# Letting an account of the array's use order TensorE's queue ahead of the experts of a hybrid block

## The chip, the core and the metric

The kernel runs on one core of a Trainium2 chip. Its engines work side by side and are tied by semaphores: TensorE (PE in the rows; PEld are its weight loads), VectorE (DVE), ScalarE (ACT), GpSimd (POOL), and SyncE (SP), which issues nearly all transfers. Each engine works through its own queue in order. The metric is the device time of one execution in microseconds (us).

## What is computed

One decoder block on 256 tokens of width 1024, in float32. One projection of x feeds an RWKV-7 time mixing (8 heads of 64), an attention (8 heads of 64) and two gates per channel; their gated sum goes through `w_out`, a residual and a layer norm. Then each token goes to 4 of 32 experts, each with 12 MB of weights.

```python
proj = jnp.einsum('btd,dc->btc', x, w_in)          # 5376 columns: rwkv 1792, attention 1536, gates 2048
y_rwkv = rwkv7_time_mix(p_rwkv, ...) @ w_branch_rwkv
y_attn = moba_attention(q, k, v) @ w_branch_attn
merged = gates[:, :, 0] * y_rwkv + gates[:, :, 1] * y_attn
x = layer_norm(DEEPNORM_ALPHA * x + merged @ w_out, ln1_g, ln1_b)
x = layer_norm(DEEPNORM_ALPHA * x + moe_ffn(x, ...), ln2_g, ln2_b)   # top 4 of 32 experts
```

The recurrence of the time mixing runs over time, `S = S * w + (S @ -kk) (kk * a) + v k`; the kernel does it in two blocks of 128 tokens, for which the inverse of a triangular 128 x 128 matrix per head and block is needed.

## The kernel before

**Stages.** The mixer comes first, to about 246 us of the profiled execution; then the branch products, `w_out`, the first norm, the router and the gathering, to about 303 us; then the experts, two to a pair, whose weights stream through a ring of ten slots (21 pieces of 1 MB), and a short end with the second norm. The slots are carved from memory that the mixer uses until its tiles are free; `stream(n)` issues the transfers up to the n-th piece, on SP's queue. The last slots become free when the output products and the router are done.

**Products of x.** The projection is made in 21 jobs of 256 columns. For a job, 2 x 512 KB of `w_in` are fetched into `wr` (four buffers), and each half is split into a high and a low part (`wh` by ACT, L211; `wl` by POOL for the first half and DVE for the second, L212; three buffers each). Then come 16 steps of three matmuls (`three`; rows `g<-xh,wh`, `g<-xl,wh`, `g<-xh,wl` or with the operands the other way round). Each step ends in `yield 0.0`.

**Half 0 and half 1 of the RWKV heads** (`rwkv_half`): decay and gates, the norm of k (a product with `bones` in `cf`), the transposes of v, b and k (`w<-ident,va`, `w<-ident,bk`), four units that make the masked 128 x 512 score blocks `sc_t` (two matmul groups, two masked copies by DVE, L531, each; a unit takes two of the four buffers of `work()`), the inverse of 16 x 16 blocks by a chain of substitution steps on DVE (L542 to L558) and four copies by ACT (L561), its transposes (`w<-ident,ring` or `w<-ident,kr`), the merges of blocks 16 to 32, 32 to 64 and 64 to 128 (many small matmuls of 64 x 32 to 64 x 64, L583 to L623), the state in two steps b = 0 and 1 (L628 to L682), and the head norm (two products with `cf`, the second for the variance; root by ACT, L698; reciprocals and products by DVE, L702 to L704). Half 1 may not begin its units before half 0's state is done.

**Attention** runs in two halves as well: per pair of heads the scores (`a<-ak,aq`), the softmax on DVE and ACT (L736 to L743), the transposes of the scores (`a<-ident,sm`), a copy by ACT (L749) and the weighted sums (`a<-sm,rope_t`).

**What sets the order.** These are Python generators: half 0, half 1, attention, and the jobs of products (`gemms`). Each `yield` gives back a number of us until the generator may go on, from the table `WAIT`, or a job and a wait after it. A loop (L828 to L847) runs the first generator that is ready by a clock of its own, `spent`, to which every matmul adds its planned time (`mm`, `turned_`); when two steps of the first three have run in a row (`FILL`), a step of products goes next. Every instruction on TensorE is tied behind the one before (`queued`). When no generator is ready, `spent` jumps. `next_job` keeps the last gate job until the first three generators are done, fetches a job's weights and, by `done` times, calls `stream`. DVE, ACT and POOL get their work in an order that follows from this program.

Of the kernel before, what the change touches and what calls it, by code (L numbers as in the profile page):

```python
# [9 lines left out]
F32 = mybir.dt.float32  # L10
# [28 lines left out]
        "sm": 3.6, "tr": 0.81, "s1": 13.02}  # L39

FILL = 2

EARLY_GATES = 3
LATE_GATES = 1
# [75 lines left out]
def hybrid_block_kernel(ctx: ExitStack, tc: tile.TileContext, A, out):  # L120
# [139 lines left out]
    ea, sq, kk, k2 = (half_t[:, i * 512:(i + 1) * 512] for i in range(4))  # L260


    def mm(out, lhsT, rhs, **k):
        n = int(np.prod(rhs.shape[1:]))
        if rhs.dtype != F32:
            spent[0] += n / 2400
        elif rhs.shape[0] <= 64:
            spent[0] += max(n, 64) / 1200
        else:
            spent[0] += max(n, int(np.prod(lhsT.shape[1:]))) / 600  # L270
        return queued("pe", nc.tensor.matmul, out, lhsT=lhsT, rhs=rhs, **k)

    def turned_(out, in_, identity):
        spent[0] += 0.107
        return queued("pe", nc.tensor.transpose, out=out, in_=in_, identity=identity)

# [136 lines left out]
    def rwkv_half(hf):  # L413
# [169 lines left out]
        for h in range(2):  # L583
# [1 line left out]
            for u in range(8):  # L585
                mm(pz[hv[h], u * 32:(u + 1) * 32], lhsT=sc_t[hv[h], u, hv[h]], rhs=first_cols(xm, h)[:, u], start=True, stop=True)
            nc.scalar.copy(out=first_cols(zt, h), in_=quarter(pz, hv[h], 32).rearrange("p u (g s) -> p u g s", s=16))
        yield WAIT["mg"]
        for h in range(2):
            pxt, px = work(), work()  # L590
            for u in range(8):
                mm(pxt[hv[h], u * 32:(u + 1) * 32], lhsT=zt[hv[h], u, hv[h]], rhs=second_cols(xt, h)[:, u], start=True, stop=True)

            n = 2 - h
            r = slice(64 * h, 64 * h + 32 * n)
            for u in range(8):
                mm(px[r, u * 16 * n:(u + 1) * 16 * n], lhsT=xt[hv[h], u, r], rhs=first_cols(zt, h, n)[:, u], start=True, stop=True)
            mask = cm[r, None, M_LEV + 64 * h:M_LEV + 64 * h + 32 * n].rearrange("p u (g s) -> p u g s", s=32)[:, :, :, 0:16]
            nc.vector.copy_predicated(out=first_cols(xm[r], 0, n) if h == 0 else xm[r, :, 64:80].rearrange("p u (g s) -> p u g s", s=16), mask=mask.to_broadcast([32 * n, 8, n, 16]), data=quarter(px, r, 16 * n).rearrange("p u (g s) -> p u g s", s=16))
            mask = cm[hv[h], None, M_LEV + P + 64 * h:M_LEV + P + 64 * h + 64].rearrange("p u (g s) -> p u g s", s=32)[:, :, :, 16:32]  # L600
            nc.vector.copy_predicated(out=second_cols(xt, h), mask=mask.to_broadcast([64, 8, 2, 16]), data=quarter(pxt, hv[h], 32).rearrange("p u (g s) -> p u g s", s=16))
        yield WAIT["mg2"]

        for size, pairs in ((32, 2), (64, 1)):
            lo_ = [slice(2 * size * g, 2 * size * g + size) for g in range(pairs)]
            hi_ = [slice(2 * size * g + size, 2 * size * g + 2 * size) for g in range(pairs)]
            for g in range(pairs):
                pz = work()
                for u in range(8):
                    mm(pz[hi_[g], u * size:(u + 1) * size], lhsT=sc_t[lo_[g], u, hi_[g]], rhs=xm[lo_[g], u, lo_[g]], start=True, stop=True)  # L610
                nc.scalar.copy(out=zt[hi_[g], :, lo_[g]], in_=quarter(pz, hi_[g], size))
            yield WAIT["mg"]
            for g in range(pairs):
                pxt = work()
                for u in range(8):
                    mm(pxt[lo_[g], u * size:(u + 1) * size], lhsT=zt[hi_[g], u, lo_[g]], rhs=xt[hi_[g], u, hi_[g]], start=True, stop=True)
                if size == 32 and g == 0:
                    px = work()
                    for u in range(8):
                        mm(px[hi_[g], u * size:(u + 1) * size], lhsT=xt[hi_[g], u, hi_[g]], rhs=zt[hi_[g], u, lo_[g]], start=True, stop=True)  # L620
                    nc.vector.tensor_copy(out=xm[hi_[g], :, lo_[g]], in_=quarter(px, hi_[g], size))
                nc.scalar.copy(out=xt[lo_[g], :, hi_[g]], in_=quarter(pxt, lo_[g], size))
            yield WAIT["mg"]  # L623

        late_a, late_b = (buf(n).rearrange("p (i c) -> p i c", i=2) for n in ("va2", "bk"))
        y_t, sq2, rstd, yn = (t[:, i, :] for t in (late_a, late_b) for i in range(2))
# [197 lines left out]
    def at(n):  # L824
        r = ready[n]
        return done.get(r[0], 1e9) + r[1] if isinstance(r, tuple) else r

    tasks = [rwkv_half(0), second_half(), halves_of(attention_half), gemms()]  # L828
    ready = [0.0] * 4
    since = 0  # L830
    while min(at(n) for n in range(3)) < 1e9 or "gate7" not in done:
        n = min((n for n in range(4) if at(n) <= spent[0]), default=None)
        if n is None:
            spent[0] = min(at(n) for n in range(4))
            continue
        if n < 3 and since >= FILL and at(3) <= spent[0]:
            n = 3
        wait = next(tasks[n], 1e9)
        since = 0 if n == 3 else since + 1
        if wait is None and min(at(i) for i in range(3)) <= spent[0]:  # L840
            wait = 0.0
        if wait is None:

            spent[0] = max(spent[0], min(at(n) for n in range(3)))
            wait = 0.0
        ready[n] = wait if isinstance(wait, tuple) else spent[0] + wait
# [776 lines left out]
```

## Time and profile before

| | us |
|---|---|
| median of 3 runs | 1240.23 |
| lowest, highest | 1227.66, 1240.44 |
| the profiled execution | 1235.69 |
| its span, first to last instruction | 1233.8 |

| share of the span | PE | PEld | DVE | ACT | POOL |
|---|---|---|---|---|---|
| busy | 93% | 47% | 33% | 21% | 8% |

[...] The profile cuts the span into slices of 31 us; the first ten are the mixer, the branches and the router, the other thirty the experts. A busy share there mixes stages with different limits, so the rows below are taken stage by stage: windows give the busy time of each engine and the granted clock of a stretch, timelines the instructions of one engine in order of time, with the idle time before them and what ended it.

### The profile page before, as it was taken

To read this page: it belongs to the slowest core of one execution; us is meant where nothing else is said; L and a number is where in the kernel's file an instruction comes from. 1 tells how busy PE (TensorE), PEld (TensorE's weight loads), DVE (VectorE), ACT (ScalarE), POOL (GpSimd) and SP (SyncE) were. 2 spreads that over 40 slices of the span, in tenths; PEclk is the share of its full clock that TensorE was granted. 3 is DMA by queue.
4 is the path that set the end of the run, shared out by engine and by line. 5 is a ranking of instruction groups with operands and counts; after the bars stand their busy time and mean duration, and the time that the engine had idled before them with its cause. 6 is when DMAs were issued, how large, how long until landed. Compare 5 with 4: busy or idle time off the path is not lost.

```text
span 1233.8 us, 15101 instructions
## 1 busy us (share of the span) xinstructions
PE 1147.7 (93%) x6396; PEld 582.5 (47%) x6396; DVE 403.3 (33%) x767; ACT 264.0 (21%) x486; POOL 97.0 (8%) x75
## 2 busy tenths in 40 slices
PE   9889979999999999999989887799998998989996
PEld 7778869888334343433424223234342333333323
DVE  6974693385522223122202011112112121212123
ACT  7455425544111110101111000011010101010111
POOL 3321121152300000000000000000000000000001
PEclk9998899999999999999999998899999999999999
DMA  8434145487999999999999999999999999999993
GB/s 269 128 95 151 56 153 172 156 318 277 397 428 427 427 426 427 429 426 427 429 427 427 428 426 426 427 427 428 427 429 426 427 428 428 428 426 427 427 420 130
DMA packets 62271, 439.79 MB, mean 356 GB/s; under 512 B 5662, under 2 KB 34168, under 8 KB 37528
## 3 DMA queue, kind: packets, MB, share of 16 engines
q1 hardware_dynamic: 60904, 427.18, 84.4%
q0 software_dynamic: 864, 11.27, 2.3%
q8 instruction: 52, 0.85, 0.3%
q10 hardware_dynamic: 432, 0.33, 0.1%
q14 instruction: 19, 0.16, 0.0%
HBM read 437.71 MB, written 1.05 MB: 356 GB/s over the span
## 4 chain that ended last, share of the span: by engine, by line
issue 34%; DMA 31%; PE 25%; DVE 7%; ACT 1%; POOL 1%; SPq 0%; POOLq 0%; ACTq 0%; DVEq 0%
DMA ring<-in_expert_w_in_dram 19%; DMA ring<-in_expert_w_out_dram 10%; PE w L132 7%; PE g L132 6%; PE h L132 5%; PE y L132 3%; PE a L132 2%; PE t L132 1%; DVE ring L554 1%; DMA acc<-in_expert_b_in_dram 1%; DVE wl L212 1%; PE t L1118 1%; DMA wr<-in_w_out_by_rows_dram 1%; DVE m L132 0%; POOL acc L1217 0%
## 5 line engine op out<-in xcount | busy, mean ns | idle before, releaser
L132 PE MATMUL h<-ring,xg 128*64 128x512 f32 x2048 | 461.4, 599 | 26.0 <-DMA ring<-in_expert_w_in_dram 25.2
L132 PEld LDWEIGHTS h<-ring,xg 128*64 128x64 f32 x2048 | 143.6, 137 | 308.8 <-issue 282.1
L132 PE MATMUL y<-ring,at 128*64 128x512 f32 x992 | 223.3, 599 | 22.8 <-DMA ring<-in_expert_w_out_dram 20.9
L1317 DVE TENSOR_SCALAR h<-h 128x512 f32<-128x512 f32 x32 | 22.4, 700 | 386.6 <-PE h L132 386.6
L132 PEld LDWEIGHTS y<-ring,at 128*64 128x64 f32 x992 | 69.2, 137 | 163.7 <-issue 134.4
L1318 ACT ACTIVATE lc<-h 128x512 f32<-128x512 f32 x32 | 19.1, 597 | 501.2 <-DVE h L1317 501.2
L132 PE MATMUL g<-xh,wh 128*128 128x256 f32 x304 | 95.4, 314 | 2.8 <-ACT rope_s L710 2.1
L1352 DVE TENSOR_TENSOR acc<-acc,t 128x512 f32<-128x512 f32 x56 | 38.5, 688 | 167.9 <-PE t L132 167.9
L132 PE MATMUL g<-xh,wl 128*128 128x256 f32 x304 | 87.9, 289 | 1.7 <-DVE wl L212 1.5
L132 PE MATMUL g<-xl,wh 128*128 128x256 f32 x304 | 87.3, 287 | 0.0
L1341 ACT COPY yp<-y 64x512 f32<-64x512 f32 x62 | 35.9, 579 | 207.6 <-PE y L132 207.0
L132 PEld LDWEIGHTS g<-xh,wh 128*128 128x128 f32 x304 | 59.4, 195 | 12.4 <-issue 8.1
L1118 PE MATMUL t<-oh,x 128*128 128x128 f32 x480 | 59.0, 282 | 6.3 <-DVE oh L1104 6.3
L1118 PEld LDWEIGHTS t<-oh,x 128*128 128x128 f32 x480 | 56.2, 196 | 18.1 <-issue 17.7
L132 PEld LDWEIGHTS g<-xl,wh 128*128 128x128 f32 x304 | 59.5, 196 | 2.2 <-issue 2.2
L132 PEld LDWEIGHTS g<-xh,wl 128*128 128x128 f32 x304 | 59.4, 195 | 2.4 <-DVE wl L212 1.7
L132 PE MATMUL t<-yp,ct 128*128 128x512 f32 (+1 forms) x124 | 56.5, 598 | 0.7 <-ACT yp L1341 0.7
L212 POOL TENSOR_TENSOR wl<-wr,wh 128x1024 fp32r<-128x1024 f32 x18 | 43.2, 2400 | 139.5 <-ACT wh L211 126.4
L211 ACT CAST wh<-wr 128x1024 fp32r<-128x1024 f32 (+1 forms) x44 | 42.2, 969 | 46.7 <-PE g L132 34.5
L132 POOL TENSOR_TENSOR acc<-acc,x 128x256 f32<-128x256 f32 x4 | 3.9, 992 | 486.9 <-DVE ln_rs L132 486.8
L132 PEld LDWEIGHTS t<-yp,ct 128*128 128x128 f32 x124 | 22.3, 189 | 34.5 <-issue 32.3
L1121 ACT ACTIVATE xg<-t,gbc 128x128 f32<-128x128 f32 x60 | 27.4, 457 | 42.4 <-PE t L1118 24.8
(375 smaller groups left out, 1075.7 us busy)
## 6 DMA issues: line engine op xcount, KB each, us to landing
ring<-in_expert_w_in_dram SPq DMA_DIRECT2D x122, 2048.0 KB, 37.0
ring<-in_expert_w_out_dram SPq DMA_DIRECT2D x61, 2048.0 KB, 39.1
wr<-in_w_in_dram SPq DMA_DIRECT2D x40, 512.0 KB, 3.9
ring<-in_expert_w_in_dram POOLq DMA_DIRECT2D x5, 2048.0 KB, 30.1
wr<-in_w_out_by_rows_dram SPq DMA_DIRECT2D x8, 512.0 KB, 4.8
ring<-in_expert_w_out_dram SPq DMA_DIRECT2D x4, 1024.0 KB, 26.4
wr<-in_w_branch_attn_dram SPq DMA_DIRECT2D x4, 512.0 KB, 7.3
wr<-in_w_branch_rwkv_dram SPq DMA_DIRECT2D x4, 512.0 KB, 9.3
```

The costliest lines, as they stand in the source:

```text
L132: queues[e] = make(*a, **k)
L211: nc.scalar.copy(out=hi[:, sl], in_=raw[:, sl])
L212: engine.tensor_tensor(out=lo[:, sl], in0=raw[:, sl], in1=hi[:, sl].bitcast(F32), op=ALU.subtract)
L554: nc.vector.tensor_tensor(out=pr[:, 0:m, 0:n], in0=nn[:, j + 1:SUB, j:j + 1].to_broadcast([P, m, n]), in1=xb[:, j:j + 1, 0:n].to_broadcast ...
L1118: last = nc.tensor.matmul(ps[:, i * ns:(i + 1) * ns], lhsT=x1[:, b, k * P:(k + 1) * P], rhs=oh[:, b, :], start=b == 0 and i == 0, stop=b = ...
L1121: def scaled(ps, n, k0, put=lambda e, make, **a: make(**a)):
L1317: nc.vector.tensor_scalar(out=gate_, in0=gate_, scalar1=7.0, scalar2=None, op0=ALU.min)
L1318: nc.scalar.activation(out=lc4, in_=g4, func=AF.Sigmoid, scale=1.702)
L1341: nc.scalar.copy(out=yp[r0_:r0_ + CAP, dh * 512:(dh + 1) * 512], in_=y[dh * CAP:(dh + 1) * CAP, :])
L1352: nc.vector.tensor_tensor(out=acc[:, b, hs], in0=acc[:, b, hs], in1=ps, op=ALU.add)
```

## The change

The planner now keeps a list of what each matmul uses of the array: in `mm`, the planned time of its columns times the share of the 128 x 128 array that its operands fill; in `turned_`, the time of a transpose. `in_use()` sums the list over the last `STRETCH` us of the planner's clock and divides by `STRETCH`. When a step of the halves or the attention is due and `in_use()` is below `FULL`, a step of products goes first, unless the last try found the products dry. Beside that, the merges have more and shorter steps: each half or pair of blocks now ends with a `yield` of its own, with a wait of 0 except the last.

```diff
+STRETCH = 3.4
+FULL = 0.65
...
+    def in_use():
+
+        while used and used[0][0] < spent[0] - STRETCH:
+            used.pop(0)
+        return sum(u for _, u in used) / STRETCH
+
     def mm(out, lhsT, rhs, **k):
         n = int(np.prod(rhs.shape[1:]))
+        m = int(np.prod(lhsT.shape[1:]))
+        used.append((spent[0], n / (600 if rhs.dtype == F32 else 2400) * min(rhs.shape[0] * m / (P * P), 1.0)))
...
     def turned_(out, in_, identity):
+        used.append((spent[0], 0.107))
...
             nc.scalar.copy(out=first_cols(zt, h), in_=quarter(pz, hv[h], 32).rearrange("p u (g s) -> p u g s", s=16))
-        yield WAIT["mg"]
+            yield WAIT["mg"] if h else 0.0
         for h in range(2):
             pxt, px = work(), work()
...
+            yield 0.0
             n = 2 - h
...
-        yield WAIT["mg2"]
+            yield WAIT["mg2"] if h else 0.0
...
-            yield WAIT["mg"]
+                yield WAIT["mg"] if g == pairs - 1 else 0.0
             for g in range(pairs):
                 pxt = work()
...
-            yield WAIT["mg"]
+                yield WAIT["mg"] if g == pairs - 1 else 0.0
...
-        if n < 3 and since >= FILL and at(3) <= spent[0]:
+        if n < 3 and (since >= FILL or in_use() < FULL and not dry) and at(3) <= spent[0]:
             n = 3
         wait = next(tasks[n], 1e9)
-        since = 0 if n == 3 else since + 1
+        since, dry = (0, wait is None) if n == 3 else (since + 1, False)
```

The table of numbers says little of where the instructions land, so three places of the order follow. First, TensorE at the second state step of half 0, before: weighted sums and scores of the attention (`a<-sm,rope_t`, `a<-ak,aq`), one product (`g`), and the state's matmuls (`w<-s` and `w<-ring_63,sc_t`).

```order
L132 MATMUL a<-sm,rope_t 64x128 x3
L132 MATMUL a<-ak,aq 128x128
L132 MATMUL a<-ak,aq 128x256
L132 MATMUL g<-xh,wh 128x256
L132 MATMUL g<-xl,wh 128x256
L132 MATMUL g<-xh,wl 128x256
L132 MATMUL w<-s_1317,ring_62 128x64
L132 MATMUL w<-ring_63,sc_t 128x64
```

The same place in the changed kernel.

```order
L135 MATMUL g<-xh,wl 128x256
L135 MATMUL a<-sm,rope_t 64x128 x3
L135 MATMUL a<-ak,aq 128x128
L135 MATMUL a<-ak,aq 128x256
L135 MATMUL w<-s_1340,ring_62 128x64
L135 MATMUL w<-ring_63,sc_t 128x64
```

The product that stood between the scores and the state now stands ahead of both. Second, DVE between half 0's head norm (`RECIPROCAL ring_62`) and half 1's masked copies (`COPY_PREDICATED sc_t`), before; between them stand rotary operations (`aq`, `rope_t`), the bonus (`nrm`), a weight split (`wl`) and others.

```order
L702 RECIPROCAL ring_62<-ring_62 128x256
L704 TENSOR_TENSOR ring_64<-ring_62,ring_63 128x256
L703 TENSOR_TENSOR ring_62<-ring_62 128x256
L212 TENSOR_TENSOR wl<-wr,wh 128x1024
L704 TENSOR_TENSOR ring_64<-ring_62,ring_63 128x256
L501 TENSOR_TENSOR nrm<-w,va_888 128x512
L716 TENSOR_TENSOR aq<-rope_s,cf 128x512
L717 TENSOR_TENSOR rope_t<-a,cf 128x512
L689 SCALAR_TENSOR_TENSOR nrm<-nrm,vec,g_t 128x256
L718 TENSOR_TENSOR aq<-aq,rope_t 128x512
```

The same place in the changed kernel.

```order
L705 TENSOR_SCALAR g_t<-g_t,vec 128x256 x2
L215 TENSOR_TENSOR wl<-wr,wh 128x1024
L717 RECIPROCAL ring_62<-ring_62 128x256 x2
L718 TENSOR_TENSOR ring_62<-ring_62 128x256 x2
L719 TENSOR_TENSOR ring_64<-ring_62,ring_63 128x256 x2
L545 COPY_PREDICATED sc_t<-cm,w 128x512 x8
```

The head norm of half 0 now stands directly ahead of half 1's copies, and the rotary operations have moved behind them. Third, TensorE at the end of the mixer in the changed kernel: the last scores, the variance product of half 1 (`w<-va_2188,cf`), the transposes of the last scores (`a<-ident,sm`) and their weighted sums; 16 products and then the branch products follow.

```order
L135 MATMUL a<-ak,aq 128x256
L135 MATMUL g<-xh,wh 128x256
L135 MATMUL g<-xl,wh 128x256
L135 MATMUL g<-xh,wl 128x256
...
L135 MATMUL w<-va_2188,cf 128x512
L135 MATMUL a<-ident,sm 128x128 x3
L135 MATMUL a<-sm,rope_t 64x128 x3
```

Three steps of products stand between the scores and the variance product. Before, the attention ended earlier, and the variance product stood alone ahead of the last 16 products:

```order
L132 MATMUL a<-sm,rope_t 64x128 x3
L132 MATMUL w<-va_2231,cf 128x512
L132 MATMUL g<-xh,wh 128x256
L132 MATMUL g<-xl,wh 128x256
L132 MATMUL g<-xh,wl 128x256
```

The last weighted sums moved from ahead of the head norm's first product, with six products behind that, to behind its second.

## Rows read from the trace of the kernel before

**Rows 1.** The chain that ended last: start us, us, what.
```profile
241.03 5.63 PE g L132 x48
...
1158.90 40.46 DMA ring<-in_expert_w_out_dram
```

**Rows 2.** Windows: stretch, us, busy PE to POOL, clock, DMA share, GB/s.
```profile
240.00:277.00 37.00, 35.64 (x284) 33.66 (x283) 30.30 (x39) 20.07 (x29) 17.52 (x14) 1.00 0.91 329
303.00:1199.00 896.00, 840.65 (x3999) 323.50 (x3998) 194.01 (x364) 106.42 (x195) 13.95 (x13) 0.99 1.01 425
```

**Rows 3.** Timeline of SP, first expert transfers: start us, us, what.
```profile
297.54 1.28 SPq L132 DMA_DIRECT2D ring<-in_expert_w_out_dram  x3
```

**Rows 4.** Waits of SP, 0 to 340 us: total us, times, longest.
```profile
SPq L132 <- PE w L132: 10.4, 1, 10.4
```

**Rows 5.** Waits of TensorE, 84 to 250 us: total us, times, longest.
```profile
PE g L132 <- DVE wl L212: 5.1, 2, 3.6
PE w L132 <- DVE sc_t L531: 1.1, 1, 1.1
```

**Rows 6.** Windows around the stretches at the low clock.
```profile
90.00:102.00 12.00, 12.00 (x125) 11.41 (x124) 4.42 (x8) 2.98 (x9) 2.38 (x1) 0.57 0.68 244
123.00:135.00 12.00, 12.00 (x65) 9.72 (x64) 8.27 (x14) 4.63 (x13) 0.95 (x1) 0.72 0.06 22
156.00:165.00 9.00, 7.89 (x44) 5.95 (x44) 6.92 (x12) 1.03 (x1) 0.95 (x1) 0.81 0.78 302
225.00:234.00 9.00, 9.00 (x55) 7.50 (x53) 2.11 (x5) 3.67 (x12) 0.00 (x0) 0.81 0.01 2
```

**Rows 7.** Timeline of TensorE: start us, us, line, instruction, count.
```profile
92.30 5.89 PE L132 MATMUL w<-ring 64*64 64x32 f32 x64
...
141.09 1.02 PE L132 MATMUL w<-ring,cf 128*128 128x512 f32 x2
...
147.94 1.02 PE L132 MATMUL w<-ring,cf 128*128 128x512 f32 x2
...
149.68 1.02 PE L132 MATMUL a<-rope_s,cf 128*128 128x512 f32 x2
...
192.08 1.03 PE L132 MATMUL w<-ident,kr 128*128 128x128 f32 x8
...
224.21 0.39 PE L132 MATMUL g<-xh,wh 128*128 128x256 f32 x1
...
225.13 0.43 PE L132 MATMUL w<-s,ar 64*128 64x64 f32 x2
...
227.94 0.56 PE L132 MATMUL g<-xh,wh 128*128 128x256 f32 x1
```

**Rows 8.** Timeline of ACT.
```profile
143.55 0.69 ACT L698 ACTIVATE ring<-w,eps_g 128x512 f32<-128x512 f32 x1
...
186.97 2.60 ACT L561 COPY kr<-ring 32x256 f32<-32x256 f32 x4 [7.58 <-DVE ring L558]
...
241.66 1.28 ACT L698 ACT_TABLE_LOAD   x1
```

**Rows 9.** Timeline of DVE.
```profile
144.27 1.75 DVE L702 RECIPROCAL ring<-ring 128x256 f32<-128x256 f32 x1 [1.52 <-ACT ring L698]
...
146.24 0.42 DVE L703 TENSOR_TENSOR ring<-ring 128x256 f32<-128x256 f32 x1
...
148.24 0.36 DVE L704 TENSOR_TENSOR ring<-ring,ring 128x256 f32<-128x256 f32 x1
...
163.17 1.37 DVE L531 COPY_PREDICATED sc_t<-cm,w 128x512 f32<-128x512 uint8 x2 [2.05 <-PE w L132]
...
178.98 2.44 DVE L554 TENSOR_TENSOR ring<-ring 128x55 f32<-128x55 f32 x1
...
186.22 0.71 DVE L558 STREAM_TRANSPOSE ring<-ring 128x512 f32<-128x512 f32 x1
...
226.68 0.35 DVE L743 TENSOR_SCALAR sm<-sm,st 128x256 f32<-128x256 f32 x1
```

More of the change, by code (lines that the diff above doesn't have):

```diff
@@ L260, in hybrid_block_kernel @@
     ea, sq, kk, k2 = (half_t[:, i * 512:(i + 1) * 512] for i in range(4))
+    used = []
+    def in_use():
+        while used and used[0][0] < spent[0] - STRETCH:
+            used.pop(0)
+        return sum(u for _, u in used) / STRETCH
     def mm(out, lhsT, rhs, **k):
         n = int(np.prod(rhs.shape[1:]))
+        m = int(np.prod(lhsT.shape[1:]))
+        used.append((spent[0], n / (600 if rhs.dtype == F32 else 2400) * min(rhs.shape[0] * m / (P * P), 1.0)))
         if rhs.dtype != F32:
@@ L269, in mm @@
         else:
-            spent[0] += max(n, int(np.prod(lhsT.shape[1:]))) / 600
+            spent[0] += max(n, m) / 600
         return queued("pe", nc.tensor.matmul, out, lhsT=lhsT, rhs=rhs, **k)
     def turned_(out, in_, identity):
+        used.append((spent[0], 0.107))
         spent[0] += 0.107
@@ L829, in hybrid_block_kernel @@
     ready = [0.0] * 4
-    since = 0
+    since, dry = 0, False
     while min(at(n) for n in range(3)) < 1e9 or "gate7" not in done:
```

## The prediction, made blind

> **What bounds the kernel now.** I read the chain that ended last first: its late part is expert weights landing one behind the other, the last at 1158.90 + 40.46 = 1199.4 us [rows 1]. The windows say the same: from 303 to 1199 us the DMA share is 1.01 at 425 GB/s [rows 2]. So the expert part has a fixed length, and the end moves with the moment at which its transfers run without a gap. SP issues the first of these at 297.54 us [rows 3], after a wait of 10.4 us for TensorE [rows 4]: the ring slots they need lie where the last output products still read. TensorE gets there through one in-order queue, so whatever it saves or loses ahead of 297 us should arrive at the end one for one. [...] It waits: 1.1 us for DVE's masks and 5.1 us for DVE's weight splits [rows 5]. [...] A row's mean gives the time lost if TensorE is the limit: (1 - 0.57) x 12 = 5.2 us, (1 - 0.72) x 12 = 3.4, and (1 - 0.81) x 9 = 1.7 twice.
>
> **What the change moves.** No instruction is added or removed on TensorE. A "product" below is one step of the generator of x's products, three matmuls; 16 of them take 5.63 us [rows 1], so one is 0.35 us at the full clock. There are 336 in both programs. Counting them ahead of each landmark in the printed orders: the first merge of half 0 still stands behind 152; the variance product of half 0 behind 200 instead of 193; the first unit of half 1 behind 204 instead of 216; the transposes after half 1's substitution behind 263 instead of 278; the last variance product behind 320 in both. So products move from the setup of half 1 into the merges of half 0, and from the substitution into the tail.
>
> *Merges of half 0: 0 us.* Up to the fourth product after the first merge matmuls the order is the same, and the clock fell by then: the 64 small matmuls at 92.30 took 5.89 us, 92 ns each [rows 7]. Two products now stand inside that block and five behind it, but the fall is not prevented, and these products run at the low clock themselves. Bounds: gain of 5.2 if the clock holds, loss of 1.7 if it stays low for one more stretch of the smaller size in [rows 6].
>
> *State steps of half 0: 0 us.* Before, one product stood between the score products and the state's second step, where the clock fell. Now none does: the first excerpt of the order shows the scores directly ahead of eight small matmuls. The new rule only asks between steps of a generator, and this step was not cut. Bounds: -3.4 to +1.7.
>
> *Half 1 begins earlier: -3.8 us.* Before, half 0's variance product starts at 141.09 [rows 7]. Now it has 7 more products ahead (2.5 us) and half 1's bonus product and eight transposes (147.94 to 149.68, 1.7 us), and one set of attention transposes and weighted sums less (about 1.1 us): 144.2. From there to the end of ACT's root took 143.55 + 0.69 - 141.09 = 3.15 us [rows 8]. Then DVE does two reciprocals of 1.75 us and four short operations of about 0.4 [rows 9], 5.1 us, all of which the new order of DVE places ahead of half 1's eight masked copies (second excerpt). So the copies start at 152.4; two took 1.37 us [rows 9], eight take 5.2, and since a unit takes two of the four buffers of its pool, the third unit must wait for the first two copies. TensorE reaches it at about 150.4 and waits until 153.7: 3.3 us where it was 1.1. The fourth unit at the low clock, as such a wait brought it before (0.81, [rows 6]), puts the last copy at 158.0, against 163.17 + 1.37 = 164.5. From there the substitution is DVE's own chain: to the end of the transpose at 186.22 + 0.71 it is 22.4 us, with two weight splits and three rotary operations between in both orders; then ACT's four copies, 2.6 us [rows 8]. So the transposes of half 1 start at 183.0 instead of 192.08 [rows 7]: -9.1 us. TensorE's 54 products there (19 us) and what it waits for splits lie under DVE's 25 us. But 15 products that stood ahead now stand behind, +5.3. Bounds: -6 (no low clock at the units) to 0 (the transposes wait for a split as before).
>
> [...]
>
> *State steps of half 1: +1.7 us.* Before, two products stood ahead of the eight small matmuls of the second step (225.13) and three behind (227.94); the clock fell there once (0.81). Now one product, weighted sums, scores and eight more small matmuls follow them. I take one more stretch of 1.7 us; bounds -1.7 (it holds) to +3.4.
>
> *The end of the mixer: +4.7 us.* The last 16 products are kept for the end in both programs, so nothing fills the attention's last waits. Before, the last weighted sums stood 22 products ahead of the end. Now the last scores are followed by three products, the variance product, and at once the transposes and the weighted sums (third excerpt). Scores ended at 224.21 and their softmax at 226.68 + 0.35 = 227.0 [rows 7, 9]: 2.8 us, of which 1.6 are filled. The turned scores must be copied by ACT, in whose queue a table load of 1.28 and the root of 0.69 [rows 8] now stand ahead of that copy: it ends about 4.9 us after the scores, where TensorE's own work ends at 1.9. So 3.0 us of waiting, and as a wait of 1.1 us brought the clock down before, 1.7 more for the products behind it. Bounds: 0 to +4.7.
>
> **Sum.** -3.8 + 1.7 + 4.7 = +2.6 us. The profiled execution took 1235.69 us (span 1233.8 and 1.9 around it), so 1238.3 us. That execution lies 4.5 us below the median of the three runs (1240.23), which spread from 1227.66 to 1240.44, so the forecast is within their spread.
>
> [...]
>
> **Rivals.**
> 1. *The clock holds, as the change's account of use intends.* For it: the falls stand at stretches of small tiles, and products now stand within merges. Against: the two places where it fell in the states have the same small matmuls or more in a row. It would give -5.2 - 3.4 - 1.7 - 3.8 + 3.0 = -11.1: about 1225 us.
> 2. *Slower: products spent early leave the tail bare.* The place is the attention of half 1, which starts two merges later. For it: its softmax and the copies behind it now stand on the path at the end; if the low clock lasts longer in the states (+3.4) and half 1's transposes gain nothing because the first products behind them wait for their split (0 instead of -3.8), it is 3.4 + 4.7 = 8 us, about 1244. Beyond 12 us it needs two more stretches at the low clock.
> 3. *Hidden anyway.* The branch stage, 240 to 277 us, has a DMA share of 0.91 [rows 2]; if its weights, not TensorE, set its end, a shift of a few us is absorbed: 1236. Against it: TensorE is busy 35.6 of 37 us there.
>
> **How the numbers follow.** I give the forecast (1232 to 1243) 0.55, rival 1 0.15, rival 2 0.2, rival 3 0.1. The predicted time is the forecast's, 1238. The range, 1226 to 1250, takes in rival 1 nearly whole and rival 2 with two more stretches, and the runs' own spread. A measurement of this kernel can tell about 1% (12 us) from no change. Faster than that needs rival 1 and more: 0.09. Slower needs rival 2 with both extras or a wait I have not seen: 0.13. Within 1%: 0.78.
>
> **What would show it.** The clock in 90 to 102 us still near 0.6; a wait of 3 us before half 1's third unit, on the masked copies; half 1's transposes near 183 us; waits of 3 us in front of the last attention products; the gapless stretch of expert transfers starting near 300 us. I am wrong if the clock stays at 1.00 through merges and states, or if SP's first expert transfer of [rows 3] does not move with TensorE.

## The result, and the profile after

The changed kernel takes 1244.86 us (median of 20 executions, 1236.42 to 1249.59) where the kernel before takes 1232.56 beside it (1225.45 to 1243.67): a ratio of 1.0081, 95% interval 1.0058 to 1.0103. Two later samples of it gave 1.0116 (1.0078 to 1.0154) and 1.0059 (1.0028 to 1.0090). So it is slower, by 7 to 14 us. Forecast were 1238 us, 2.6 more than before, and no change that can be told; the time lies in the range given, the difference is one that can be told. The profiled execution took 1242.07 us, its span is 1240.2: 6.4 us more than before. Four single executions of the samples below, 1249.0 to 1256.4 us at a mean granted clock of 0.961 to 0.965, lie over 1.5% above the fastest of their kernel and count as slow; ratios and means leave them out.

The first rows of the changed kernel answer [rows 3] and [rows 2]: SP's first gapless expert transfer, and the windows of the expert part.

```profile
303.92 1.28 SPq L135 DMA_DIRECT2D ring<-in_expert_w_out_dram  x3
```
```profile
core 0: us, PE busy (x) PEld busy (x) DVE busy (x) ACT busy (x) POOL busy (x), PEclk, DMA share, GB/s
309.00:1199.00 890.00, 833.63 (x3979) 321.27 (x3980) 193.58 (x365) 106.26 (x195) 14.34 (x14) 0.99 1.01 426
```

It starts at 303.92 instead of 297.54, 6.4 us later, and the span is 6.4 us longer: from there to the end both kernels take 936.3 us. All that is to be explained lies ahead of the experts.

The windows of the changed kernel that answer [rows 6] (the columns are the stretch, its length, TensorE's busy time with its instructions, granted clock, DMA share, GB/s):

```profile
core 0: us, PE busy (x), PEclk, DMA share, GB/s
87.00:102.00 15.00, 15.00 (x190) 1.00 0.26 72
102.00:123.00 21.00, 21.00 (x227) 1.00 0.58 201
123.00:135.00 12.00, 12.00 (x84) 1.00 0.15 45
147.00:156.00 9.00, 8.80 (x39) 0.62 0.12 33
171.00:177.00 6.00, 6.00 (x39) 0.72 0.87 325
189.00:210.00 21.00, 21.00 (x179) 0.51 0.27 101
221.00:240.00 19.00, 19.00 (x147) 1.00 0.07 28
240.00:246.00 6.00, 3.94 (x24) 1.00 0.00 0
```

The same window of the kernel before, for half 1's merges:

```profile
189.00:210.00 21.00, 21.00 (x271) 0.97 0.59 202
```

Half 0's merges and states, at 0.57 and 0.72 before, run at 1.00. Half 1's merges (189 to 210), at 0.97 before, run at 0.51 with TensorE busy all the time. It looks as if the change had moved the fall from half 0 to half 1. That reading was my first theory (A), and it did not hold.

TensorE's timeline of the changed kernel: half 1's transposes (before at 192.08, [rows 7]), the first scores of half 1's attention (before 1.0 us behind those transposes), and the last two attention steps, with the wait ahead of them in brackets.

```profile
179.75 1.04 PE L135 MATMUL w<-ident,kr 128*128 128x128 f32 x8
...
211.19 0.92 PE L135 MATMUL a<-ak,aq 64*128 64x128 f32 x4
...
242.22 0.70 PE L135 MATMUL a<-ident,sm 128*128 128x128 f32 x3 [0.43 <-DVE sm L757]
244.54 0.87 PE L135 MATMUL a<-sm,rope_t 128*64 128x128 f32 x6 [1.63 <-ACT sm L764]
```

Half 1's transposes come 12.3 us earlier, with 15 products (5.3 us) fewer ahead of them. The other 7 us are not won by the new order: half 0 alone lost 5.2 + 3.4 us to the clock in [rows 6] and loses nothing here (more in the step by step part). And half 1's attention begins 31.4 us behind the transposes. The cause is an exchange of two jobs, seen in the order in which the planner starts them: before, `aq1` (q of half 1's attention) begins at product 192 and the third gate at 208; with the change the gate begins at 192 and `aq1` at 208, `ak1` at 240 instead of 224, `av1` at 272 instead of 256. The rule puts products ahead of attention's steps too; half 0's attention so ends later, `aq1` is asked for only at product 206 (before at 187), and by then the gate has begun. A job once begun runs through its 16 products. The traces show the exchange: ACT's copy of `aq1` starts at 148.32 us before, ahead of the gate at 166.33, and at 160.33 with the change, behind the gate at 152.40.

### The profile page after: what moved, and what is told of

The parts are those of the page before. It is cut to its first block, busy times and chain, and to the rows that moved or that the text cites. A ratio compares the mean times of both kernels' runs of the same rounds, so it can differ in the third digit from the quotient of the medians.

```text
span 1240.2 us, 15099 instructions
## 1 busy us (share of the span) xinstructions
PE 1151.7 (93%) x6396; PEld 584.7 (47%) x6396; DVE 403.2 (33%) x767; ACT 264.1 (21%) x486; POOL 97.9 (8%) x75
## 3 DMA queue, kind: packets, MB, share of 16 engines
HBM read 437.71 MB, written 1.05 MB: 354 GB/s over the span
## 4 chain that ended last, share of the span: by engine, by line
issue 34%; DMA 29%; PE 27%; DVE 6%; ACT 2%; POOL 1%; SPq 0%; POOLq 0%; ACTq 0%; DVEq 0%
DMA ring<-in_expert_w_in_dram 16%; DMA ring<-in_expert_w_out_dram 10%; PE w L135 7%; PE h L135 6%; PE g L135 6%; PE y L135 3%; PE t L135 2%; PE a L135 1%; DVE ring L569 1%; DMA acc<-in_expert_b_in_dram 1%; PE t L1133 1%; DVE wl L215 1%; DMA wr<-in_w_out_by_rows_dram 1%; DMA wr<-in_w_branch_attn_dram 1%; DVE ring L568 1%
```

## The experiments

Each ratio is to runs of the kernel before on the same chip; 12 executions of the kernel in question unless said otherwise and 23 to 35 of the kernel before, interval 95%. The times in the expectations go by 1232.6 us for the kernel before; its medians beside the runs differ by chip (1232.4 to 1237.8), so the ratios are what to compare. A theory's letter is the one in the quoted expectations.

**Parts and halves.** The rule alone (the merge steps as before):

```diff
-            yield WAIT["mg"] if h else 0.0
+        yield WAIT["mg"]
```
(and the four other yields likewise)

> The planner's rule alone; the merges keep their old long steps. Base: 1232.6 us before, 1244.9 us with the whole change. Theory A (the loss is TensorE's clock at 0.50 over about 19 us of half 1's merges, 191 to 210 us, because what stands there is thin): with long merge steps there is less for the rule to go between, so half 0's merges fall again (about 5 us lost, as before the change) and half 1's fall too: 1240 to 1250. Theory B (the loss is in waits of TensorE that the rule makes by taking the products from the places where they covered a wait: 2.0 us at the units, 1.8 at the splits, 1.1 at the rope, 2.1 at the end): the waits are the same, so 1240 to 1246, with merges of half 1 at 1.00. Theory C (where the clock falls differs from run to run, and the change only shifts it): anything between 1232 and 1245, and the low stretch elsewhere.

1239.27 us, 1.0050 (1.0018 to 1.0082). Half 1's merges ran at 1.00; 17 us of its state steps, 217 to 234, did not. That is under the range of theories A and B and inside that of C; the merges at 1.00 are as B has it.

The short steps alone:

```diff
-        if n < 3 and (since >= FILL or in_use() < FULL and not dry) and at(3) <= spent[0]:
+        if n < 3 and since >= FILL and at(3) <= spent[0]:
```

> The shorter merge steps alone; the planner keeps its count of two steps to a product. Theory A: two merge steps between products are now half as long, so half 0's merges hold more of their clock (mean over 90 to 102 us above 0.8 where it was 0.57 before), and half 1's merges, with their attention steps still among them, keep 1.00: 1226 to 1231. Theory B: no product moves far, so no new wait of more than 1 us, and with no clock gain counted 1231 to 1235. Theory C: 1228 to 1240, with the low stretch in one or the other half.

1240.68 us, 1.0066 (1.0026 to 1.0105). Theory A expected a gain here, and the time lies above all three ranges. The jobs start in the old order and half 1's transposes stand 1.0 us ahead of attention as before, so neither the rule nor late attention is needed for a loss of this size.

The change in one half alone (the condition of the rule, put together from the two edits; the short steps are bound to the same half):

```diff
+ (since >= FILL or "state0" not in done and in_use() < FULL and not dry)    # short steps where hf == 0
+ (since >= FILL or "state0" in done and in_use() < FULL and not dry)        # short steps where hf == 1
```

> The whole change for half 0 alone: the rule until half 0's state is done, the shorter steps in half 0's merges; half 1 by the old rule and the old steps. Theory A: half 0's gain stays (about 8.6 us of clock, less some 4 us of waits and low clock behind them at half 1's units), and half 1's merges keep 1.00 as before the change: 1225 to 1231, mean clock of the 20 us behind half 1's identity transposes above 0.95. Theory B: the waits of half 1's units and splits come from products taken early, and are still there: 1234 to 1242. Theory C: half 1's merges fall here too although nothing is changed in them: 1234 to 1244.

1239.63 us, 1.0054 (1.0023 to 1.0084). Theory A falls: half 1's merges kept 1.00 from 180 to 210 us, and it is as slow. TensorE reached the end of half 1's RWKV part at 229 us and waited for attention:

```profile
engine line waited for: us in total, times, longest us
PE a L135 <- DVE sm L762: 5.7, 1, 5.7
```

> The whole change for half 1 alone: the rule from half 0's state on, the shorter steps in half 1's merges; half 0 by the old rule and the old steps. Theory A: half 0 runs as before the change (clock about 0.57 over its first merges) and half 1's merges fall: 1238 to 1246, 6 to 12 us above before. Theory B: only the waits at the end of the mixer and at the splits, some 2 to 4 us: 1234 to 1237, half 1's merges at 1.00. Theory C: 1230 to 1244, not told from before.

1241.12 us, 1.0048 (1.0016 to 1.0079); half 1's merges at 0.50 from about 198 to 229 us. So what A says can happen, but it is not all of the loss: either half alone costs more than half of the whole.

**The job order.** The whole change, and q of half 1's attention asked for when half 0's attention reaches its last two heads; and the kernel before with nothing but the gate ahead of q:

```diff
         for c in range(2):
+            if (hf, c) == (0, 1):
+                asked_rope("aq1", ATT0 + 256, 0.125)
```
```diff
-        if asked:
-            asked.sort(key=lambda a: a[0][0] == "a")
+        asked.sort(key=lambda a: a[0][0] == "a")
+        if asked and not (asked[0][0] == "aq1" and len(free_gates) == 6):
```

> The whole change, and beside it the product for the q of half 1's attention is asked for when half 0's attention reaches its last two heads, so that it goes ahead of the third gate's product, as it did before the change (with the change that gate goes first, and half 1's attention begins one job of 16 products later: its first scores stand at 211 us where they stood at 193). Theory D (the loss comes from half 1's attention starting late: its steps are missing among half 1's merges, which are thin and fall to 0.50, and stand bare at the end): attention among the merges again, no wait over 1 us at the mixer's end, 1231 to 1237. Theory A (the loss is the low clock in half 1's merges, made by the shorter steps and the rule there): 1240 to 1246, low stretch at half 1's merges as with the change. Theory C (chance of the clock): 1234 to 1245 with the low stretch anywhere.

1240.01 us, 1.0030 (0.9998 to 1.0062), beside 1.0116 for the change on the same chip: most of the loss in this pair, but theory D's 1231 to 1237 is missed. The later pair of the same two kernels, below, lies only 0.0023 apart.

> The kernel before the change, with one thing of it alone: the third gate's product goes ahead of the q product of half 1's attention. No rule, no shorter steps. Theory D: half 1's attention starts one job late here too, 2 to 4 us bare at the mixer's end and thinner merges: 1236 to 1242. Theory A: the order of the two jobs is no matter: 1231 to 1235.

1237.29 us, 1.0014 (0.9976 to 1.0052). The time is in theory D's range, but the kernel before took 1237.76 on this chip. By itself the exchange costs nothing that can be told: attention then begins 15.2 us behind the transposes, not 24 to 31 as with the change.

The change in half 0 alone, with the same added lines for `aq1`:

> The change for half 0 alone (as in the run of that name, 1239.6 us, where TensorE stood 5.7 us bare before the last softmax), with the q product of half 1's attention ahead of the third gate. Theory D: half 0's clock gain stays, and the bare 5.7 + 1.1 us at the mixer's end go: 1229 to 1234. Theory E (what is won in half 0 is always given back, since the products that fill half 0 are missing later: idle and low clock together stay at 33 to 36 us): 1236 to 1242, with the low clock or the wait at another place of half 1.

1234.03 us, 0.9990 (0.9959 to 1.0022), where the gate first gave 1.0054: about what theory D expected.

**The same kernels again.**

> The changed kernel as it is, for a second profile. If the order of the instructions sets where the clock falls, the stretch at 0.50 stands in half 1's merges again (190 to 210 us) and half 0's merges hold 1.00: 1242 to 1247. If it is chance (theory C), the low stretch is elsewhere or of another length, by 3 us or more.

1249.26 us (6 executions), 1.0116 (1.0078 to 1.0154). In this profile half 1's merges keep 0.92, and half 1's state steps fall. The third profile, from a later run, is like it; its windows:

```profile
171.00:177.00 6.00, 5.37 (x43) 1.00 0.82 306
189.00:210.00 21.00, 21.00 (x238) 0.92 0.39 132
221.00:240.00 19.00, 19.00 (x78) 0.55 0.01 1
```

> The kernel before the change once more, for a second profile. Theory C (where the clock falls is partly chance): the stretches at 0.50, which were 91 to 102, 125 to 133 and 183 to 191 us, are elsewhere or of other lengths, and the ratio is 1.000 within 0.004. If the order of the instructions sets them: the same three stretches.

1238.15 us, 1.0042 (1.0013 to 1.0072): the same program as the one it is compared with, and an interval that leaves out 1. So one sample of 12 can be off by 0.4%, and a single ratio below that tells nothing; what follows rests on two or three samples of each kernel. Its windows:

```profile
87.00:102.00 15.00, 15.00 (x194) 1.00 0.48 170
102.00:123.00 21.00, 21.00 (x223) 1.00 0.34 106
123.00:135.00 12.00, 12.00 (x86) 1.00 0.15 45
189.00:210.00 21.00, 21.00 (x227) 0.67 0.49 176
221.00:240.00 19.00, 19.00 (x88) 0.62 0.00 1
```

The kernel before, in another execution, shows what the first profile of the changed one showed: half 0 at 1.00, half 1 far below. Where the clock falls is in part a draw (theory C), and [rows 6] were one draw.

**The square.** Rule with old steps and q first, later the four corners again on one chip:

```diff
+            if (hf, c) == (0, 1):
+                asked_rope("aq1", ATT0 + 256, 0.125)      # on top of the rule alone
```

> The planner's rule alone with the old long merge steps, and the q product of half 1's attention ahead of the third gate. Beside it stand the rule alone with the gate first (ratio 1.005 to before) and the whole change with q first (1.003). Theory D (the late attention is the rule's whole cost, the short steps a second cost of their own): 0.996 to 1.000 of before. Theory F (the rule itself takes products from places where they are needed, wherever attention starts): 1.003 to 1.007.

1233.48 us, 0.9999 (0.9970 to 1.0028).

> The rule alone, old merge steps, third gate ahead of half 1's q product (first sample 1.005). If late attention costs some 6 us with the rule on: 1.003 to 1.007, and 0.003 to 0.007 above the run with q first. If the first samples were chance: within 0.002 of it.

1241.76 us, 1.0038 (1.0010 to 1.0066).

> The rule alone, old merge steps, q first (first sample 0.9999). If the rule as such costs nothing: 0.997 to 1.002. By the profile, less than 25 us at 0.50 ahead of the branch products.

1234.96 us, 0.9979 (0.9949 to 1.0010).

> The whole change with q first (first sample 1.003, beside 1.0116 for the change). If the short steps cost some 6 us by themselves: 1.003 to 1.007. If the late attention was the whole loss: 0.998 to 1.002.

1241.49 us, 1.0036 (1.0008 to 1.0064).

> The change as it is, a third profile. If the two terms add: 1.008 to 1.012, 0.004 to 0.007 above both runs that lack one of them. If the square is chance, it is no further from them than 0.002.

1244.78 us, 1.0059 (1.0028 to 1.0090). Neither range was met: it is 0.0021 and 0.0023 above the two that lack one term. On this chip the terms do not add: alone they cost 0.0059 and 0.0057, together 0.0080.

Means of the samples, all with the rule:

| | gate first | q first |
|---|---|---|
| old merge steps | 1.0044 (1.0050, 1.0038) | 0.9989 (0.9999, 0.9979) |
| short merge steps | 1.0085 (1.0081, 1.0116, 1.0059) | 1.0033 (1.0030, 1.0036) |

Read across, the gate first costs 0.0055 and 0.0052, read down, the short steps 0.0044 and 0.0041: some 6.5 and 5 us, which in these means add up to the loss. The samples come from several chips; on the one chip of the four later runs the same steps are 0.0059 and 0.0023, and 0.0057 and 0.0021. That each term is a cost is shown, that they add is not. The rule alone, with the jobs in the old order, neither costs nor gains anything that can be told in the time; what lies behind that stands in the next section.

**The short steps alone, again** (the edit of the first such run):

> The shorter merge steps alone, without the rule (first sample 1.0066). If the short steps are a cost of their own, some 6 us, by more alternations and by falls of the clock among them that last longer: 1.003 to 1.007, and a fall in either half's merges, if there is one, of 17 us or more. If the first sample was chance: 0.998 to 1.002.

1242.32 us, 1.0081 (1.0041 to 1.0121). Without the rule they cost 8 to 10 us, as much as the whole change: in two samples the clearest single part. The fall in its profile lasted from 99 to 114 us, a little short of the 17 expected; the time was above the range expected.

**Three variations.** The rule in half 0 alone, old steps, q first:

```diff
-        if n < 3 and (since >= FILL or in_use() < FULL and not dry) and at(3) <= spent[0]:
+        if n < 3 and (since >= FILL or "state0" not in done and in_use() < FULL and not dry) and at(3) <= spent[0]:
```

> The rule in half 0 alone, no shorter steps at all, q ahead of the third gate. It differs from the run with the change in half 0 and q early (0.999) in the shorter steps of half 0's merges alone. Theory G (each alternation between products and small steps costs TensorE some 0.2 us, and short steps keep a clock that has fallen down for longer): 0.994 to 0.998. If the short steps of half 0 are a gain: 1.000 to 1.004.

1234.71 us, 1.0019 (0.9985 to 1.0053), beside 0.9990 with half 0's short steps. It lies in the range that calls half 0's short steps a gain, not in theory G's, but the two intervals overlap: a cost of the short steps is not shown for half 0 alone.

The change with q first, and a higher bound:

```diff
-FULL = 0.65
+FULL = 0.9
```

> The whole change with q early (1.003), and the rule's bound at 0.9 where it was 0.65: the rule now puts products in until the last microseconds are nearly full. Theory E (the products are a fixed stock of 336 steps: what is spent in half 0 is missing in half 1): half 0's merges and states at 1.00 throughout, half 1's merges and attention without products, low clock and waits there of 10 us or more: 1.010 to 1.030. If a denser mixture is a gain by itself: below 1.000.

1263.46 us (6 executions), 1.0252 (1.0214 to 1.0290). Half 0 was paid for with the products of half 1:

```profile
87.00:131.00 44.00, 38.43 (x411) 1.00 0.48 156
...
222.00:270.00 48.00, 45.46 (x304) 0.54 0.00 1
```

The last gate's product may begin before the last softmax is through (rule, old steps, q first):

```diff
-... LATE_GATES if min(at(n) for n in range(3)) < 1e9 else 0)
+... LATE_GATES if min(at(n) for n in range(3)) < 1e9 and "last" not in done else 0)
+                if hf and c and h:
+                    done["last"] = spent[0]
-                yield WAIT["sm"]
+                yield WAIT["sm"] + (1.2 if "last" in done else 0.0)
...
-                yield WAIT["tr"]
+                yield WAIT["tr"] + (0.5 if "last" in done else 0.0)
```

> The rule, old merge steps, q first (0.9999 and 0.9979), and beside it the last gate's product may begin before the last softmax of half 1 is through, so that some 10 of its 16 products stand in the 2.6 us in which TensorE waits there. If the wait is worth its length: 2 to 3 us less, 0.996 to 0.998 of before. If the rest of the last gate no longer covers the split of the attention's output behind it: the wait moves there, 0.998 to 1.001.

1233.72 us, 0.9990 (0.9958 to 1.0023), not told from 0.9989 without it. The wait of 2.6 us is gone, and 1.6 us of it stand behind it, where the branch products now wait for the split of the attention's output:

```profile
243.60 0.39 PE L135 MATMUL a<-ring,wh 128*128 128x256 f32 x1 [1.64 <-DVE ring L926]
```

No version is shown to beat the kernel before.

## Where the time went

TensorE's time up to the first branch product, split by windows of 1 us: idle; busy time x (1 - granted clock) as the clock's loss; and the rest.

| kernel, one line per profile | idle | clock | rest | first branch product |
|---|---|---|---|---|
| before | 16.7 | 16.6 | 213.3 | 246.5 |
| before, second | 15.5 | 21.2 | 213.8 | 250.5 |
| the change | 15.4 | 20.5 | 215.2 | 251.1 |
| the change, second | 18.5 | 17.1 | 217.6 | 253.1 |
| the change, third | 18.7 | 17.0 | 217.7 | 253.4 |
| short steps alone | 16.5 | 20.1 | 215.1 | 251.6 |
| short steps alone, second | 17.9 | 15.8 | 216.7 | 250.5 |
| rule, old steps, gate first | 18.0 | 18.4 | 214.5 | 250.8 |
| the same, second | 19.7 | 13.4 | 214.3 | 247.4 |
| the change, q first | 18.0 | 13.6 | 216.4 | 248.1 |
| the same, second | 17.8 | 25.5 | 214.2 | 257.5 |
| rule, old steps, q first | 18.4 | 9.4 | 215.7 | 243.4 |
| the same, second | 19.2 | 11.9 | 215.2 | 246.3 |

**Every execution.** Two profiles of a kernel tell little of a clock that falls by a draw, but the mean granted clock of every execution is known. As an estimate, its span x (1 - mean granted clock) is what the low clock took, and the remainder of the span is all else. In 162 executions of the kernel before, time and this estimate move together (correlation 0.93), and the mean remainder of their six samples is 1203.5 to 1204.1 us. The experts' part is in both columns; the differences are what counts.

| kernel | executions | clock, us | remainder, us |
|---|---|---|---|
| before | 162 | 28.9 | 1203.8 |
| rule, old steps, q first | 24 | 23.0 | 1209.3 |
| rule, old steps, gate first | 24 | 29.4 | 1209.1 |
| the change, q first | 23 | 28.7 | 1209.8 |
| the change | 38 | 33.6 | 1209.6 |
| short steps alone | 23 | 34.3 | 1206.4 |
| rule in half 0 alone, old steps, q first | 12 | 30.8 | 1202.6 |

The standard errors are 0.4 to 1.6 us for the clock and 0.2 to 0.6 for the remainder. So the rule does what it is meant to do, 5.9 us less lost to the clock, and pays 5.5 us for it outside the clock; that is why its time does not change. With the rule in half 0 alone the remainder is not longer, so these 5.5 us come with the rule in half 1; the table of profiles has them as idle time and rest, 2.7 and 1.9 us. Theory B looked for the loss there; which waits and steps they are stays open. The gate first costs 6.4 and 4.9 us, all of it clock. The short steps cost 5.7 and 4.2 us of clock and 0.5 outside it; alone, without the rule, 5.4 and 2.6.

**The short steps, carrier 1.** In the profiles with them the rest is 214.2 to 217.7 (mean 216.1), without them 213.3 to 215.7 (mean 214.5): the ranges overlap, and the means differ by 1.7 us. An alternation between products and small matmuls had a price where I read it: from the changed kernel's timeline, a product alone between two small groups:

```profile
221.44 0.39 PE L135 MATMUL g<-xh,wh 128*128 128x256 f32 x1
221.66 0.28 PE L135 MATMUL g<-xl,wh 128*128 128x256 f32 x1
221.78 0.28 PE L135 MATMUL g<-xh,wl 128*128 128x256 f32 x1
221.98 0.34 PE L135 MATMUL w<-er,ek 128*64 128x64 f32 x4
```

From 221.44 to 221.98 it took 0.54 us where a product in a row takes 0.35 [rows 1]: 0.19 us more. Ahead of the branch products there are 51 groups of products before and with the rule alone, 57 with the change and 58 with the short steps alone: 1 us, an estimate with that one reading of 0.19; the cut merge groups would be the rest, which I did not measure alone.

**The short steps, carrier 2.** Falls among them lasted longer. In the low stretches the granted clock was 0.50, as in 92 to 101 us before and in 199.2 to 208.3 with the change, TensorE busy all the time in both. Low stretches of over 5 us that began in merges, with short steps: 189 to 210 (the change), 198 to 229 (half 1 alone), 97 to 118 and 99 to 114 (steps alone), 96 to 127 (q first, second); 23 us in the mean. With old steps: 91 to 102 (before), 92 to 103 (twice), 195 to 208 (before, second); 11 us. At 0.50 the 12 us more are some 6 us in an execution in which the clock falls there, about as much as the table of executions has. These are nine falls, falls of 3.4 us stand in the merges of both groups beside them, and one more profile (the change in half 0 alone, q first) has 21 us in half 1's old steps. So the lengths are indicated rather than measured well; the times are measured.

**The gate first.** It shows in half 1's state steps. With the rule and the gate first they had a low stretch of 17 us in four of five profiles (217 to 234, 216 to 233, 221 to 238, 222 to 239); in the fifth the merges had fallen instead. With q first all five (the four of the square and the one with the last gate moved) had 3.4 us there. The rule alone, second profile, gate first, at the fall at 216:

```profile
215.81 0.45 PE L135 MATMUL g<-xh,wh 128*128 128x256 f32 x1
216.06 0.42 PE L135 MATMUL g<-xl,wh 128*128 128x256 f32 x1
216.28 0.42 PE L135 MATMUL g<-xh,wl 128*128 128x256 f32 x1
216.63 1.54 PE L135 MATMUL a<-sm,rope_t 128*64 128x128 f32 x6
218.10 1.65 PE L135 MATMUL a<-ak,aq 64*128 64x128 f32 x4
219.68 1.97 PE L135 MATMUL w<-w_s,kr 128*128 128x64 f32 x8
```

The same place with q first, second profile:

```profile
221.94 0.38 PE L135 MATMUL g<-xl,wh 128*128 128x256 f32 x1
...
222.75 0.41 PE L135 MATMUL g<-xh,wl 128*128 128x256 f32 x1
222.97 1.80 PE L135 MATMUL w<-w_s,kr 128*128 128x64 f32 x8
224.53 0.56 PE L135 MATMUL g<-xh,wh 128*128 128x256 f32 x1
...
225.47 0.28 PE L135 MATMUL g<-xl,wh 128*128 128x256 f32 x1
```

The late attention's weighted sums and scores stand between the two groups of state products, with one product ahead of them and two behind; the clock is down until 233. With q first these attention steps lie ahead of the fall, three products come at once, and the matmuls of 0.28 us are back at 225.4. The windows say it in one number each: 215 to 234 us at 0.55 there, 0.91 here.

```profile
215.00:234.00 19.00, 19.00 (x78) 0.55 0.01 1
```
```profile
215.00:234.00 19.00, 19.00 (x129) 0.91 0.17 64
```

That the gate first costs clock is shown by the executions. That the late attention is what keeps the clock down fits these ten profiles; it was not tried by moving those steps alone, and the second profile of before fell there (225 to 243 us) without it.

## Why the prediction was wrong, step by step

- **The bound: right.** SP's first expert transfer and the span moved by the same 6.4 us. Roughly, the sum put +3.4 us on the clock (1.7 twice) and -0.8 on all else (-3.8 + 3.0). By the executions it is +4.7 and +5.8: the time outside the clock is where the sum failed most.
- **Merges and state steps of half 0, "0 us": a step that failed.** The fall was taken for something that the order makes, because up to the fourth product the order is the same. The changed kernel held 1.00 from 87 to 135 us in all three profiles; but so did the kernel before in its second. The base of the sum, (1 - granted clock) x length of the windows of [rows 6], was one execution's draw of the clock, and so was the 1235.69 us it was made against: medians of the kernel before were 1232.35 to 1238.15 in the samples here. What the edit to the steps costs was then missed altogether: bounds of -5.2 to +1.7, where the short steps of both halves cost 8 to 10 us alone and some 5 with the rule. The rule read from that one profile, that a wait of 1.1 us brings the clock down, fails with it: in the second profile of before the same wait, 1.05 us at 153.02, is followed by no fall until 178 us.
- **Half 1 begins earlier, "-3.8 us": the main step that failed, hidden by the draw.** The signs came true: the third unit waited 2.0 us for DVE's masked copies (3.3 forecast), the transposes started at 179.75 (183.0 forecast). But half 0's variance product already stood at 138.10 instead of the 144.2 forecast, as half 0 kept its clock. From the first merge of half 0 to the transposes, with the clock's loss taken out and the 15 products put back, it is 90.4 and 91.7 us in two profiles of before and 91.0, 93.4 and 93.5 with the change: no gain that shows, and in two of three profiles a loss of 2 to 3 us. That the transposes were near the forecast is luck.
- **The order of the jobs: a term that was left out.** The landmarks were counted in products, and the exchange of the third gate's job with `aq1` keeps the counts. It costs some 5 to 6.5 us, all of it clock by the executions.
- **State steps of half 1, "+1.7 us": mis-sized.** Nothing in the first profile, 17 us at the low clock, some 8 us, in the two others. The bound of +3.4 was too near.
- **End of the mixer, "+4.7 us": right in kind.** The waits stand where they were put, on the transposes and on ACT's copy (L764), but measure 0.43 + 1.63 us; behind them the clock fell for 3.4 us in two of three profiles. So 2 to 4 us. It is no cost of the late attention: with q first the wait is 2.6 us.
- **The rivals.** Rival 2 (slower, 1244 us, half 1's attention late and the tail bare) came nearest: its time is the result, and its longer low clock in the states is what two profiles show. It had 0.2 because the late start was read as "two merges later" with no reason that would lengthen it. Rival 1's condition was met in half 0 and its gain did not come: the second profile of before has the same clock there. What it describes does show in the rule with old steps and q first, 5.9 us less lost to the clock, and is paid for outside it. The products are a fixed stock besides, as `FULL = 0.9` showed.

## What to carry to other kernels

Take a second and a third profile of the kernel before pricing lost clock: a fall at one place in one execution is not a property of the order. Where a rule moves work in a planner, list the order in which whole jobs start, not only how many steps stand ahead of each landmark: one exchanged job cost as much clock here as all that the rule won. Where the clock of every execution is at hand, split a change's cost into clock and remainder: a ratio of 1.00 hid 6 us won and 5.5 lost. And filler work is a fixed stock: spending it early leaves the later stage bare.

## What the hardware showed that I had not expected

The same program's low stretches ahead of the experts add up to very different lengths: the clock's loss was 16.6 and 21.2 us in two profiles of the kernel before, in different stages, and its times spread over 1225 to 1245 us. No run here shows what sets the place of a fall.

In the changed kernel, from 189 to 210 us, TensorE stayed at 0.51 while it was busy 21.00 of 21.00 us, with runs of up to 15 matmuls of 128 x 256 among the small ones; 54 of them start in the window, some 11.5 of its 21 us. At 1.00 such matmuls follow each other every 0.12 us (240.06 to 240.65), there every 0.21. So a queue without gaps did not keep the clock there, nor did large matmuls for half of the time.
